# A hybrid mixer layer on one core: first group's solve levels moved, first rows loaded ahead of weights, weights split by whole blocks

## The chip, the core and the metric

The kernel runs on one core of one Trainium2 chip. The metric is device time in microseconds (us) of one execution. The kernel before was run three times: 2560.08, 2561.3 and 2566.76 us, median 2561.3. One more execution was taken with the hardware profiler: 2558.94 us.

A core has five engines with a queue of instructions each: TensorE (PE, matmuls, with its weight loads shown as PEld), VectorE (DVE), ScalarE (ACT), GpSimd (POOL) and SyncE (SP). Here SP issues most DMA transfers; ACT issues some too. An instruction that waits holds up all that stands behind it in its engine's queue.

## The reference

One layer of a streaming encoder: 2048 prompt rows (16 tiles of 128) and 128 sample rows (8 streams of 16, one more tile), width 1024.

```
h   = RMSNorm_pre(x);  P = h @ w_in   # [q|k|v (3*512) | z 512 | b 4 | a 4 | B 512 | C 512 | H 512]
q,k,v = SiLU(causal_conv4(..)); q,k L2-normed; beta = sigmoid(b); g = -exp(A_log)*softplus(a+dt)
per 64-row chunk, 4 heads of 128:
  A   = strictly lower (beta k k^T * decay);  [u|w] = (I + A)^-1 [beta v | beta k exp(g)]
  v_new = u - w S;  o = (q exp(g)) S + (q k^T * decay) v_new;  S = S*a_last + k_tail^T v_new
o   = RMSNorm_head(o) * SiLU(z)
y   = B * causal_conv3(C * H)
x   = x + RMSNorm_post(concat(o, y) @ w_o)
x   = x + RMSNorm_post2(SwiGLU(RMSNorm_pre2(x)))        # d_ff = 2816
```

All is fp32. The outputs are y for prompt and samples, and the new conv and delta-rule states.

## The kernel before

An fp32 matmul is made of three float32r matmuls: each operand is split into a rounded high part and a low rest, and wh·hi, wh·lo and wl·hi are summed. Making the parts is ACT's and DVE's work: ACT rounds a weight tile to `wh` (L276), DVE subtracts for `wl` (L277); rows are split by L212 (ACT, `hi`) and L213 (DVE, `lo`).

The kernel has four stages. In the mixer stage (0 to 943 us of the span) the 17 tiles go in five groups, `GROUPS = [[0,1,2],[3,4,5,6],[7,8,9,10],[11,12,16],[13,14,15]]` (16 is the sample tile). Each group runs through 28 column blocks of `w_in`, of 128 columns each. A block is 24 matmuls (8 slices of 128 rows, three each) into one PSUM bank, and its result goes through the convolutions and gates. Afterwards come the product with `w_o` (`o_tile`), the gate and up products, and the down product; the change doesn't touch the last two.

In group 0 (and for every fourth block in group 1) a block's weights come raw from `w_in`, are split, and the split pair (1 MB) is stored to a DRAM tensor `wsplit`; later groups load the pair from there. The pair sits in `w2`, a ring of three buffers; the raw tile `wr` (L275) comes as two halves of 128x512, from a ring of four. `fetch()` issues the next block's weights: once per block at its end, and at the very start in three calls between the first rows.

Before group 0 the rows `xs0` are loaded (L863, 8 slices, into tiles named `U` and `AU`), split, squared (L869 to L873), and their squares summed on TensorE (L881); the inverse norm is spread over the partitions by a TensorE transpose (L204) and scales everything that is read from a block's bank.

Everything that is not a block's matmuls (gate rates, decay masks, key products, the triangular solve, the chunks of the delta rule, loading and squaring of the next group's rows L225 to L235) is placed by `plan` between the thirds of the blocks: a block's matmuls come in three parts (9, 9 and 6), and `at(t, f)` puts `f` behind third number `t`. Distances in time are turned into thirds by `after(us)`, with 2.3 us a third in group 0 and `THIRD = {3: 1.95, 4: 2.5}` by the group's number of tiles in the others. TensorE's instructions stay in that written order. The order on the other engines is made by a scheduler.

The solve: `solve` forms the inverse of 32x32 diagonal blocks on DVE by pairs of small operations (L568, L570) on the transposed matrix `As` (L559). `solve_store` transposes the result into `utd` (L575, L576). Then `level_a` (L590, small matmuls with `utd`, L593), `level_b` (L607, L608), `level_c` (L629) and `level_d` (L640) combine the blocks, each a few TensorE instructions with DVE and ACT work between. `chunk` then runs the delta rule over the tiles; L699 is one of its matmuls, yt by dt, into an `obank`.

PSUM has eight banks: three `dbank` (blocks), two `tbank` (transposes, L342), two `gbank` (solve) and one `obank`. `out_turn` (L656) transposes a tile's result, in an `obank`; DVE reads it and multiplies by the gate (`ot`, L658); ACT issues the store to `mixo` (L659). The short convolution's result `yo` (L420) is stored to `mixs` by ACT's queue (L425).

The `w_o` stage begins with weights and rows that were loaded early (L976, L977 split them into `woh`, `wol`; L981, L982 split those loaded later, whole tiles of 128x1024). For each tile L1001 and L1002 split the mixer's rows `mh` and `ml`, and L1007 multiplies.

Of the kernel before, what the change touches and what calls it, by code (L numbers as in the profile page):

```python
# [17 lines left out]
P = 128  # L18
# [63 lines left out]
def kernel(  # L82
# [74 lines left out]
    with ExitStack() as ph:  # L157
# [21 lines left out]
        mark = {}  # L179
        early_w, early_m = [], []  # L180

# [27 lines left out]
        def split(xk, k, c, hi, lo):  # L209
            h = hp.tile([P, W1], F32R, tag="hi", name="hi")  # L210
            l = hp.tile([P, W1], F32R, tag="lo", name="lo")
            A.activation(h[:, :c], xk[:, :c], AF.Copy, scale=g_pre[:, k:k + 1])  # L212
# [50 lines left out]
        def weights(j, gi):  # L263
# [3 lines left out]
            if not (gi <= late or (gi == RAWG and j % 2)):  # L267
# [3 lines left out]
                return wh, wl  # L271
            for q in range(2):
                c = slice(4 * q, 4 * q + 4)
                wr = wp.tile([P, KD // 2, P], F32, tag="wr", name="wr", bufs=4)
                wload = nc.sync.dma_start(out=wr, in_=w_in[j, :, c])  # L275
                A.copy(wh[:, c], wr)  # L276
                V.tensor_tensor(out=wl[:, c], in0=wr, in1=wh[:, c].bitcast(F32), op=ALU.subtract)  # L277
            wloads.append(wload)
# [75 lines left out]
        def finish_block(j, ps, g):  # L354
# [62 lines left out]
            if kind == "B":  # L417
                acc = g["acc"]
                yo = cp.tile([P, W1], F32, tag="cs", name="yo")
                V.tensor_mul(yo[:, :pc], acc[:, :pc], ps[:, :pc])  # L420
# [232 lines left out]
        def out_turn(g, i, o):  # L653
            ps = obank()
            for h in range(H):
                T.transpose(ps[:, h * P:(h + 1) * P], o[:, h, :], ident)  # L656
            ot = wk.tile([P, H, P], F32, tag="ot", name="ot")
            V.scalar_tensor_tensor(ot, h4(ps), g_hd, g["sz"][:, :, i * P:(i + 1) * P], op0=ALU.mult, op1=ALU.mult)  # L658
            nc.scalar.dma_start(out=mixo[g["tiles"][i]], in_=ot)  # L659

# [106 lines left out]
        def plan(g, nx, events):  # L767
# [91 lines left out]
        hi, lo, sqs = [], [], []  # L859
        firsts = [psd.tile([P, 512], F32, tag="d", name="dbank") for _ in range(2)]  # L860
        for k in range(KD):
            raw = (U if k < 4 else AU)[:, k % 4].rearrange("p h c -> p (h c)")[:, :c]
            nc.sync.dma_start(out=raw, in_=xs0[k])  # L863
            split(raw, k, c, hi, lo)
            if k in (0, 3):
                fetch()
            sq = xbuf()
# [15 lines left out]
        rx = rstd(small, psn[:, :2 * n].rearrange("p (t c) -> p t c", c=2)[:, :, 0], n, 1.0 / D, EPS, "x")  # L883
        fetch()
        late()
        cw = gp.tile([P, 12, 4], F32, name="cw")
# [84 lines left out]
        for k in range(KD):  # L971
# [6 lines left out]
            else:  # L978
                wr = op.tile([P, D], F32, tag="xo", name="wor", bufs=2)
                nc.sync.dma_start(out=wr, in_=w_o[k])  # L980
                A.copy(wh, wr)  # L981
                V.tensor_sub(wl, wr, wh.bitcast(F32))  # L982
        nc.sync.dma_start(out=gpost, in_=rows_[0].partition_broadcast(P))

# [556 lines left out]
```

## Time and profile before

| | before |
|---|---|
| runs, us | 2560.08, 2561.3, 2566.76 (median 2561.3) |
| profiled execution, us | 2558.94 |
| its span, us | 2557.1 |
| mean granted TensorE clock | 0.99 |
| PE / DVE / ACT / POOL busy | 97 / 65 / 38 / 24 % |
| mixer stage ends (last block's matmul) | 943.3 us |

The span is the time from the first to the last recorded instruction. What the profile gives as "idle before" an instruction is the gap on its engine; the name behind the arrow is the instruction whose end released it. In the tables of waits a row is: engine, what waited (output and line), what it waited for, then total us, number of times, longest. In a timeline a row is: start in us, busy us, engine, line, operation, output and inputs, shape, and in brackets the idle time before it with its releaser. An engine name with a q is that engine's queue issuing something, such as a DMA.

### The profile page before, as it was taken

What the parts mean: (1) busy time and instruction counts of PE and PEld (TensorE: products, weight loads), DVE (VectorE), ACT (ScalarE), POOL (GpSimd) and SP (SyncE); (2) the same over time, 40 slices, a digit from 0 to 9 for tenths busy, and PEclk for the clock granted to TensorE, in tenths of its full rate; (3) what the DMA queues carried; (4) which work ended last, traced back from release to release, by engine and by line L of the source; (5) the groups of instructions that cost most, each with busy time, mean ns of one, the idle gap of its engine ahead of it and who ended that gap; (6) DMA issues with size and microseconds to landing.
All of it is one profiled execution on the core that took longest, in us unless ns stands there. A gap on an engine that the chain in (4) does not pass through costs nothing.

```text
span 2557.1 us, 39320 instructions
## 1 busy us (share of the span) xinstructions
PE 2469.6 (97%) x14366; PEld 2254.5 (88%) x14366; DVE 1667.9 (65%) x3106; ACT 976.7 (38%) x2095; POOL 607.3 (24%) x679
## 2 busy tenths in 40 slices
PE   7789999999999999999999999999999999999998
PEld 6788887888999988789999999999999987887786
DVE  6866755745755655768877764544655464677698
ACT  5435424423424323534433442222433345333343
POOL 1111010110111000215655500000000045455564
PEclk9989999999999999999999999999999999999999
DMA  6756554556667555669877888887888844333375
GB/s 231 256 209 220 180 206 179 180 172 205 232 223 254 207 182 189 210 227 340 285 261 263 283 267 262 262 252 260 284 282 294 280 152 127 95 124 123 125 226 183
DMA packets 287393, 561.91 MB, mean 220 GB/s; under 512 B 26652, under 2 KB 175328, under 8 KB 269920
## 3 DMA queue, kind: packets, MB, share of 16 engines
q1 hardware_dynamic: 165808, 483.06, 55.8%
q10 hardware_dynamic: 121392, 76.34, 9.6%
q8 instruction: 113, 1.85, 0.3%
q14 instruction: 80, 0.66, 0.1%
HBM read 400.62 MB, written 158.70 MB: 219 GB/s over the span
## 4 chain that ended last, share of the span: by engine, by line
PE 78%; DVE 11%; DMA 4%; issue 3%; ACT 2%; POOL 1%; ACTq 0%; SPq 0%; DVEq 0%; POOLq 0%
PE fbank L1223 32%; PE dbank L297 21%; PE fbank L1381 12%; PE tbank L1007 3%; PE dbank L1007 3%; DVE acc L1340 1%; DMA xt<-in_x 1%; PE tbank L342 1%; DVE acc L301 1%; DVE xr L1400 1%; PE obank L699 1%; DMA partd<-pt 1%; PE gbank L734 1%; POOL dw L1080 1%; PE obank L679 1%
## 5 line engine op out<-in xcount | busy, mean ns | idle before, releaser
L1223 PE MATMUL fbank<-xh,fw 128*128 128x384 f32 (+1 forms) x3696 | 899.2, 326 | 6.6 <-ACT m L1257 2.9
L297 PE MATMUL dbank<-hi,w 128*128 128x384 f32 (+1 forms) x2240 | 675.7, 369 | 10.7 <-ACT w L276 7.7
L1223 PEld LDWEIGHTS fbank<-xh,fw 128*128 128x128 f32 x3696 | 651.8, 188 | 8.3 <-ACT m L1257 3.6
L1223 PE MATMUL fbank<-xl,fw 128*128 128x384 f32 (+1 forms) x1848 | 602.5, 326 | 0.0
L1381 PE MATMUL fbank<-dw,as 128*128 128x512 f32 x1980 | 459.5, 393 | 8.6 <-DVE as L1365 2.7
L297 PEld LDWEIGHTS dbank<-hi,w 128*128 128x128 f32 x2240 | 418.9, 190 | 49.0 <-ACT w L276 7.6
L1381 PEld LDWEIGHTS fbank<-dw,as 128*128 128x128 f32 x1980 | 370.2, 188 | 97.7 <-DVE as L1365 4.1
L297 PE MATMUL dbank<-lo,w 128*128 128x384 f32 (+1 forms) x1120 | 404.0, 361 | 0.9 <-DVE lo L213 0.9
L1223 PEld LDWEIGHTS fbank<-xl,fw 128*128 128x128 f32 x1848 | 347.5, 188 | 0.0
L1365 POOL TENSOR_TENSOR as<-ar,as 128x256 fp32r<-128x256 f32 (+1 forms) x207 | 186.7, 912 | 277.1 <-ACT as L1362 276.4
L297 PEld LDWEIGHTS dbank<-lo,w 128*128 128x128 f32 x1120 | 213.7, 191 | 19.4 <-DVE lo L213 2.6
L1340 DVE TENSOR_TENSOR acc<-acc,fbank 128x512 f32<-128x512 f32 x248 | 166.1, 682 | 93.3 <-PE fbank L1381 75.6
L1080 POOL TENSOR_TENSOR dw<-dr,dw 128x512 fp32r<-128x512 f32 x52 | 76.8, 1489 | 484.7 <-ACT dw L1078 484.5
L1362 ACT CAST as<-ar 128x256 fp32r<-128x256 f32 (+1 forms) x288 | 118.1, 427 | 183.3 <-PE fbank L1381 135.6
L301 DVE SCALAR_TENSOR_TENSOR acc<-R,cw,acc 128x384 f32<-128x384 f32 (+2 forms) x180 | 121.2, 675 | 58.8 <-ACT acc L331 51.8
L1198 ACT CAST fw<-rg 128x512 fp32r<-128x512 f32 x124 | 77.4, 624 | 192.1 <-PE fbank L1223 154.4
L1270 DVE TENSOR_TENSOR c<-u,fbank 128x384 f32<-128x384 f32 (+1 forms) x66 | 34.8, 528 | 103.5 <-PE fbank L1223 103.4
L1266 DVE TENSOR_TENSOR m<-m,m 128x384 f32<-128x384 f32 (+1 forms) x44 | 23.1, 525 | 91.2 <-ACT m L1259 91.1
L1268 ACT ACTIVATE m<-fbank 128x384 f32<-128x384 f32 (+1 forms) x66 | 31.3, 474 | 127.6 <-PE fbank L1223 119.0
L1199 POOL TENSOR_TENSOR fw<-rg,fw 128x512 fp32r<-128x512 f32 x44 | 69.7, 1583 | 32.9 <-ACT fw L1198 32.8
L323 POOL COPY hist<-R 128x3 f32<-128x3 f32 x60 | 21.3, 355 | 190.3 <-ACT R L306 164.0
L1199 DVE TENSOR_TENSOR fw<-rg,fw 128x512 fp32r<-128x512 f32 x80 | 56.4, 706 | 15.3 <-ACT fw L1198 12.9
(359 smaller groups left out, 3476.3 us busy)
## 6 DMA issues: line engine op xcount, KB each, us to landing
w<-wsplit SPq DMA_DIRECT2D x105, 1024.0 KB, 4.9
fw<-fsplit SPq DMA_DIRECT2D x188, 512.0 KB, 4.8
fsplit<-fw SPq DMA_DIRECT2D x94, 512.0 KB, 4.2
partd<-pt ACTq DMA_DIRECT2D x88, 384.0 KB, 6.7
rg<-in_w_gu SPq DMA_DIRECT2D x62, 512.0 KB, 4.1
wsplit<-w SPq DMA_DIRECT2D x28, 1024.0 KB, 5.1
ar<-partd SPq DMA_DIRECT2D x48, 384.0 KB, 3.3
wr<-in_w_in SPq DMA_DIRECT2D x70, 256.0 KB, 5.0
```

The costliest lines, as they stand in the source:

```text
L297: T.matmul(ps[:, :c], l[:, k, :], r[k][:, :c], start=(k == 0 and r is hi and l is wh), stop=(k == KD - 1 and l is wl))
L301: r = V.scalar_tensor_tensor(acc, raw(d), w[:, d:d + 1], acc, op0=ALU.mult, op1=ALU.add)
L1007: T.matmul(pss[n], m_[:, j, :], w_[k][:, n * 512:(n + 1) * 512], start=(k == 0 and ci == 0), stop=(k == KD - 1 and ci == 2))
L1080: e.tensor_tensor(out=w[:, 1], in0=v, in1=w[:, 0].bitcast(F32), op=ALU.subtract)
L1198: A.copy(w[:, 0], v)
L1199: e.tensor_tensor(out=w[:, 1], in0=v, in1=w[:, 0].bitcast(F32), op=ALU.subtract)
L1223: T.matmul(ps, w_[:, c], b_[k][:, :hw], start=(first and k == 0 and ci == 0), stop=(k == KH - 1 and ci == 2), skip_group_check=not first)
L1270: V.tensor_add(c21, u2, b3)
L1340: V.tensor_add(dst, dst, ps)
L1362: ins = A.copy(a[:, 0, :n], v)
L1365: e.tensor_tensor(out=a[:, 1, :n], in0=v, in1=a[:, 0, :n].bitcast(F32), op=ALU.subtract)
L1381: T.matmul(ps, a[:, x_, q * P:(q + 1) * P], w[:, y_], start=(start and q == 0 and ci == 0), stop=(q == c - 1 and ci == 2), skip_group_chec ...
```

## The change

1. In group 0 the four levels stand seven thirds later. In groups of three tiles (0, 3 and 4) `level_b` stands 5 us behind `level_a` instead of 3.4, one third more; the rest follows.
2. At the start all eight row loads are issued in one go: the first block's weights behind the first slice, the second block's behind all eight. The squares come in a second loop. The other inputs (constants, convolution weights, caches, gate parameters, all by ACT's queue) are issued behind the last `hi` split.
3. A block's raw weights come as one tile of 128x1024, split by one ACT and one DVE instruction; only the first block is still done in halves. `wr` has two whole buffers in place of four halves.
4. `out_turn` transposes into a `tbank` in place of the `obank`.
5. The last group's last `mixs` store and the last tile's `mixo` store go from ACT's queue to SP's, behind the loads of `w_o`; the last `yo` gets another buffer.

On TensorE, group 0, around `level_a` of the kernel before (w_1251 is a block's weights, vraw a block of values being transposed, utd the solve's result, AU the matrix it multiplies):

```order
L297 MATMUL dbank<-lo,w_1251 128x384
L297 MATMUL dbank<-hi,w_1251 128x384
L342 MATMUL tbank<-cst,vraw 128x128 x3
L590 MATMUL gbank<-utd,AU 32x32 x24
L297 MATMUL dbank<-hi,w_1251 128x384
```

In the changed kernel the transposes of that block stand alone, and L595 (the same `level_a`) comes in a block two further on:

```order
L298 MATMUL dbank<-lo,w_1293 128x384
L298 MATMUL dbank<-hi,w_1293 128x384
L595 MATMUL gbank<-utd,AU 32x32 x24
L298 MATMUL dbank<-hi,w_1293 128x384
L298 MATMUL dbank<-lo,w_1293 128x384
```

Between the two places lie 57 block matmuls and three transposes.

On DVE, the last steps of group 0's solve before, and what stands around them (xt are squares of the next group's rows):

```order
L568 TENSOR_TENSOR pr<-As,Ts 128x108
L570 TENSOR_TENSOR Ts<-Ts,pr 128x9x12
L568 TENSOR_TENSOR pr<-As,Ts 128x96
L570 TENSOR_TENSOR Ts<-Ts,pr 128x8x12
L568 TENSOR_TENSOR pr<-As,Ts 128x91
L570 TENSOR_TENSOR Ts<-Ts,pr 128x7x13
L233 TENSOR_SCALAR xt,xss<-xt 128x512
L568 TENSOR_TENSOR pr<-As,Ts 128x78
L570 TENSOR_TENSOR Ts<-Ts,pr 128x6x13
```

After, the same steps (L573 and L575 are the solve's pair):

```order
L573 TENSOR_TENSOR pr<-As,Ts 128x108
L575 TENSOR_TENSOR Ts<-Ts,pr 128x9x12
L233 TENSOR_SCALAR xt,xss<-xt 128x512
L278 TENSOR_TENSOR w_1387<-wr,w_1387 128x1024
L573 TENSOR_TENSOR pr<-As,Ts 128x96
L302 TENSOR_SCALAR acc<-u,scw,acc 128x384
L575 TENSOR_TENSOR Ts<-Ts,pr 128x8x12
L302 TENSOR_SCALAR acc<-u,scw,acc 128x384
L573 TENSOR_TENSOR pr<-As,Ts 128x91
L233 TENSOR_SCALAR xt,xss<-xt 128x512
L575 TENSOR_TENSOR Ts<-Ts,pr 128x7x13
```

More of the blocks' own work stands between the solve's steps. Counted from `As` to `utd`: 9 weight subtractions of 128x1024 in place of 14 of 128x512, and in addition two taps of 128x384 (L302 with scw), one `vt`, one `cs`, one `u`, one `xt` square, one spread of 128x512 (L201) and two tiny ones.

The start of SP's queue before (U and AU take the rows, wr raw weights):

```order
L863 DMA U<-in_xs 128x384
L275 DMA wr<-in_w_in 128x512 x2
L863 DMA U<-in_xs 128x384 x3
L275 DMA wr<-in_w_in 128x512 x2
L282 DMA wsplit_82<-w_224 128x2048
L863 DMA AU<-in_xs 128x384 x4
L275 DMA wr<-in_w_in 128x512 x2
```

And after:

```order
L874 DMA U<-in_xs 128x384
L276 DMA wr<-in_w_in 128x512 x2
L874 DMA U<-in_xs 128x384 x3
L874 DMA AU<-in_xs 128x384 x4
L276 DMA wr<-in_w_in 128x1024
L283 DMA wsplit_82<-w_220 128x2048
L276 DMA wr<-in_w_in 128x1024
```

The four `AU` loads no longer stand behind the store of the first split block, nor behind the second block's weights.

```diff
-            for q in range(2):
-                c = slice(4 * q, 4 * q + 4)
-                wr = wp.tile([P, KD // 2, P], F32, tag="wr", name="wr", bufs=4)
-                wload = nc.sync.dma_start(out=wr, in_=w_in[j, :, c])
-                A.copy(wh[:, c], wr)
-                V.tensor_tensor(out=wl[:, c], in0=wr, in1=wh[:, c].bitcast(F32), op=ALU.subtract)
+            wr = wp.tile([P, KD, P], F32, tag="wr", name="wr", bufs=2)
+            parts = 1 if wloads else 2
+            for q in range(parts):
+                c = slice(KD // parts * q, KD // parts * (q + 1))
+                wload = nc.sync.dma_start(out=wr[:, c], in_=w_in[j, :, c])
+                A.copy(wh[:, c], wr[:, c])
+                V.tensor_tensor(out=wl[:, c], in0=wr[:, c], in1=wh[:, c].bitcast(F32), op=ALU.subtract)
...
-                nc.scalar.dma_start(out=mixs[g["gi"]][:, h, :], in_=yo[:, :c])
+                if last:
+                    last_stores.append((mixs[g["gi"]][:, h, :], yo[:, :c]))
+                else:
+                    nc.scalar.dma_start(out=mixs[g["gi"]][:, h, :], in_=yo[:, :c])
...
         def out_turn(g, i, o):
-            ps = obank()
+            ps = tbank()
...
+            if not gi:
+                t += 7
             for f in (level_a, level_b, level_c, level_d):
                 at(t, f, g)
-                t += after(3.4)
+                t += after(5 if f is level_a and n < MAXT else 3.4)
...
             nc.sync.dma_start(out=raw, in_=xs0[k])
+            raws.append(raw)
+            if not k:
+                fetch()
             split(raw, k, c, hi, lo)
-            if k in (0, 3):
-                fetch()
+        fetch()
+        for k, raw in enumerate(raws):
             sq = xbuf()
...
+        inputs = ExitStack()
+        inputs.enter_context(tc.issue_after(started))
         late()
...
+        inputs.close()
...
+        for a, b in last_stores:
+            nc.sync.dma_start(out=a, in_=b)
```

More of the change, by code (lines that the diff above doesn't have):

```diff
@@ L179 @@
         mark = {}
-        early_w, early_m = [], []
+        early_w, early_m, last_stores = [], [], []
         inner = ph.enter_context(ExitStack())
@@ L211, in split @@
             l = hp.tile([P, W1], F32R, tag="lo", name="lo")
-            A.activation(h[:, :c], xk[:, :c], AF.Copy, scale=g_pre[:, k:k + 1])
+            mark["hi"] = A.activation(h[:, :c], xk[:, :c], AF.Copy, scale=g_pre[:, k:k + 1])
             V.scalar_tensor_tensor(l[:, :c], xk[:, :c], g_pre[:, k:k + 1],
@@ L418, in finish_block @@
                 acc = g["acc"]
-                yo = cp.tile([P, W1], F32, tag="cs", name="yo")
+                last = h == 3 and g["gi"] + 1 == len(GROUPS)
+                yo = wk.tile([P, W1], F32, tag="ye", name="yo") if last else cp.tile([P, W1], F32, tag="cs", name="yo")
                 V.tensor_mul(yo[:, :pc], acc[:, :pc], ps[:, :pc])
@@ L658, in out_turn @@
             V.scalar_tensor_tensor(ot, h4(ps), g_hd, g["sz"][:, :, i * P:(i + 1) * P], op0=ALU.mult, op1=ALU.mult)
-            nc.scalar.dma_start(out=mixo[g["tiles"][i]], in_=ot)
+            if i + 1 < g["npr"] or g["gi"] + 1 < len(GROUPS):
+                nc.scalar.dma_start(out=mixo[g["tiles"][i]], in_=ot)
+            else:
+                last_stores.append((mixo[g["tiles"][i]], ot))
         def tail_keys(g, i):
@@ L860 @@
         firsts = [psd.tile([P, 512], F32, tag="d", name="dbank") for _ in range(2)]
+        raws = []
         for k in range(KD):
@@ L884 @@
         fetch()
+        started = mark["hi"].ins
+        inputs = ExitStack()
+        inputs.enter_context(tc.issue_after(started))
         late()
```

## The prediction, made before the changed kernel ran

> **What bounds the kernel now.** I read the page first: busy shares, TensorE's row in 40 slices, the granted clock.
>
> ```profile
> span 2557.1 us, 39320 instructions
> PE 2469.6 (97%) x14366; PEld 2254.5 (88%) x14366; DVE 1667.9 (65%) x3106; ACT 976.7 (38%) x2095; POOL 607.3 (24%) x679
> PE   7789999999999999999999999999999999999998
> PEclk9989999999999999999999999999999999999999
> ```
>
> TensorE is the bound; 2557.1 − 2469.6 = 87.5 us of the span lie between its matmuls. A slice is 64 us, and only the first three and the last are not full. So all that this change can win is idle time of TensorE, mostly in the first 192 us, and it adds no matmul. The waits of TensorE over the whole span name the places.
>
> ```profile
> engine line waited for: us in total, times, longest us
> PE gbank L590 <- DVE utd L575: 14.2, 2, 13.9
> PE obank L699 <- DVE ot L658: 7.8, 7, 2.1
> PE dbank L297 <- ACT w L276: 7.7, 1, 7.7
> ...
> PE dbank L1007 <- ACT mh L1001: 5.9, 2, 3.7
> ...
> PE gbank L607 <- ACT xs L593: 2.3, 1, 2.3
> ```
>
> Five parts of the change each aim at one of these rows. I take them in the order of the program.
>
> **The start.** The timeline of the first 31 us:
>
> ```profile
> 2.11 2.71 SPq L863 DMA_DIRECT2D U<-in_xs  x3
> 7.00 1.26 ACT L276 CAST w<-wr 128x512 fp32r<-128x512 f32 x2
> 7.65 0.69 PE L297 MATMUL dbank<-hi,w 128*128 128x384 f32 x1 [7.65 <-ACT w L276]
> 9.79 5.72 SPq L863 DMA_DIRECT2D AU<-in_xs  x4
> 14.71 0.20 ACT L901 ACTIVATE nega<-al 128x4 f32<-128x4 f32 x1 [2.60 <-DMA al<-in_gates]
> 15.65 0.61 ACT L212 ACTIVATE hi<-AU,vec 128x384 fp32r<-128x384 f32 x1
> 16.31 0.69 PE L297 MATMUL dbank<-hi,w 128*128 128x384 f32 x1 [2.86 <-ACT hi L212]
> 30.49 1.48 PE L204 MATMUL tbank<-xk,cst 128*128 128x384 f32 x2
> ```
>
> The rows of the second half (AU) are issued only at 9.79, behind the store of the first split block, which itself waits for DVE's subtraction. So the first block, begun at 7.65, stands in its middle until 16.31. ACT, which must split those rows, spends 2.6 us waiting for `al`, a small gate input.
>
> In the changed kernel SP issues the AU rows right behind U's three, at about 2.11 + 2.71 = 4.8 us. All rows (8 x 196 KB), the first weights (512 KB) and the start's other loads had this rate to come at:
>
> ```profile
> 4.00:6.00 2.00, 0.00 (x0) 0.00 (x0) 0.00 (x0) 1.23 (x1) 0.00 (x0) 1.00 0.95 323
> ```
>
> At 323 GB/s, 2.1 MB need 6.5 us; with some 2 us ahead of the first byte the rows are there at about 8.5. ACT then has eight `hi` at 0.61, three squares at about 0.5 and two half casts (1.26), 7.7 us from about 6, so the last `hi` ends near 13.7 and the first block near 14.5. The second block's weights now wait for ACT: behind the last `hi` stand three DMA issues and one whole cast. They are ready near 17, the block ends near 21, and L204 stands near 25 in place of 30.49: 5.5 us. Against that, `al` is still issued from ACT's queue, ahead of the third block's cast, and the fourth block's cast and subtraction (1.05 + 1.23, whole tiles, below) now stand ahead of the first taps. I take 1.5 off: **4 us**, bounds 1 (ACT's queue gives most of it back) and 7 (L204 at 23.5, no loss).
>
> What the rate is under two queues the trace shows in part: in that window the engines are 95% busy. The Trainium skill, "DMA: Bandwidth & Descriptors", section "Queues, rings and completion order", says that a DMA engine takes turns between its queues packet by packet; by it, moving ACT's constants behind the last `hi` gives the rows a larger share of the engines, which would put the start's gain nearer to 5.5. The row of 323 GB/s agrees with busy engines, and no row separates the queues' shares.
>
> **Levels of group 0.** The largest single hole, with DVE's prices in the first 160 us:
>
> ```profile
> 91.99 2.12 DVE L559 STREAM_TRANSPOSE As<-pk 128x1024 f32<-128x1024 f32 x1 [2.76 <-ACT pk L557]
> 120.99 0.55 PE L342 MATMUL tbank<-cst,vraw 128*128 128x128 f32 x3
> 134.38 1.06 DVE L575 STREAM_TRANSPOSE utd<-Ts 128x512 f32<-128x512 f32 x1
> 135.49 1.49 PE L590 MATMUL gbank<-utd,AU 32*32 32x32 f32 x48 [13.95 <-DVE utd L575]
> L277 DVE TENSOR_TENSOR w<-wr,w 128x512 fp32r<-128x512 f32 x44 | 30.2, 704 | 8.1 <-ACT w L276 7.9
> L301 DVE SCALAR_TENSOR_TENSOR acc<-R,cw,acc 128x384 f32<-128x384 f32 x36 | 21.7, 610 | 2.6 <-ACT acc L333 1.9 <-POOL hist L323 0.5
> L233 DVE SCALAR_TENSOR_TENSOR xt<-xt 128x512 f32<-128x512 f32 x4 | 2.7, 687 | 2.2 <-DMA xt<-in_x 2.2
> ```
>
> TensorE reaches the level at 121.54, that is 29.55 us behind the start of `As`; `utd` ends 43.45 us behind it (135.44). Seven thirds later means 57 more block matmuls, by the order. A block's 24 matmuls and three transposes take 4.85 us here (two such transposes start at 116.14 and 120.99), so 57 and three need some 10.3: TensorE arrives at +39.85. But TensorE's extra blocks bring DVE extra work, which the scheduler puts between the solve's steps: nine whole subtractions for fourteen halves, 9 x 1.23 − 14 x 0.704 = 1.2 us (the 1.23 is a whole subtraction, row below); two taps, 1.2; `vt`, `cs` and `u` at 0.55, 1.65 (as `yo`, of the same shape, in the last timeline below); one square 0.69 and one spread, also 128x512, 0.69; a little for two tiny ones: 5.7 us. `utd` then ends at +49.15, and the remaining hole is 9.3 us. A fourth square joins the three whose loads DVE waited 2.2 us for, so I leave 10: the gain is **4 us**, not the 13.95 that the move might suggest. Bounds: 0 (the squares wait longer, `As` itself comes later) and 6.9 (those 2.2 us gone: 7.1 left).
>
> Behind the hole the clock drops:
>
> ```profile
> 120.00:140.00 20.00, 5.91 (x66) 5.29 (x66) 13.16 (x41) 7.91 (x18) 0.78 (x3) 0.60 0.53 186
> 136.91 0.69 PE L297 MATMUL dbank<-hi,w 128*128 128x384 f32 x1
> 141.21 0.34 PE L297 MATMUL dbank<-lo,w 128*128 128x384 f32 x1
> ```
>
> Thirteen matmuls start from 136.91 up to 141.21, 0.33 us apart, where those ahead start (4.85 − 0.55)/24 = 0.18 apart: 13 x 0.15 = 1.9 us. With 10 us of hole left I save none of it. "TensorE: Matmul & The Clock Gate" of the Trainium skill, section "Part 1: The HAM clock gate", lets the clock fall after about 3.4 us of idle time; by that, the 1.9 us would come on top only with the hole under 3.4. The trace agrees so far that 13.95 us drop it (granted clock 0.60).
>
> **Level b in groups of three.** L607 waits 2.3 us, once, for `xs`; nine more matmuls stand ahead of it: 9 x 0.18 = **1.6 us**, bounds 0 and 2.3.
>
> **Outputs in transposition banks.** DVE's reading of the output bank, over the mixer stage (min/median/max in ns):
>
> ```profile
> L658 DVE SCALAR_TENSOR_TENSOR ot<-obank,vec,sz x17: 743/746/753, 179.9 to 942.2; 128x512 f32<-128x512 f32 x17
> ```
>
> L699 waits 7.8 us in seven places for DVE's reading of the one `obank`. With `out_turn` elsewhere that reader is gone. A transpose (L342) may now find its `tbank` held by the output until `ot` has read it, 0.75 us a time; there are two banks, and the row for `obank` counts seven of 17 tiles as late. I take **7 us**, bounds 2 (each of seven waits turns into up to 0.75 us on a `tbank`, and one in ten is new) and 7.8.
>
> **Whole-block splits.** Rows on both sides:
>
> ```profile
> L276 ACT CAST w<-wr 128x512 fp32r<-128x512 f32 x44 | 25.7, 617 | 34.9 <-PE dbank L297 19.6 <-DMA wr<-in_w_in 9.6 <-issue 4.8
> 953.30 1.05 ACT L981 CAST woh<-wor 128x1024 fp32r<-128x1024 f32 x1 [3.35 <-DMA wor<-in_w_o]
> 954.38 1.23 DVE L982 TENSOR_TENSOR wol<-wor,woh 128x1024 fp32r<-128x1024 f32 x1 [2.89 <-ACT woh L981]
> ```
>
> Whole is cheaper on the engines (1.05 for 2 x 0.617, 1.23 for 2 x 0.704). A block's weights become ready later by half a cast and half a load, some 1.5 us, and a load now needs a whole tile free. The cover is the ring of three: before, ACT's cast mostly waits for TensorE to give a buffer back (19.6), not for the load (9.6), and after the start TensorE waits for no `w`. **0**, bounds −3 and +25 us (third rival).
>
> **The end of the mixer stage.**
>
> ```profile
> 943.30 0.55 DVE L420 TENSOR_TENSOR yo<-acc,dbank 128x384 f32<-128x384 f32 x1 [0.30 <-PE dbank L297]
> 944.27 0.62 ACT L976 CAST woh<-U 128x512 fp32r<-128x512 f32 x1 [4.37 <-DVE yo L420]
> 944.92 0.69 DVE L977 TENSOR_TENSOR wol<-U,woh 128x512 fp32r<-128x512 f32 x1 [1.06 <-ACT woh L976]
> 947.02 0.79 PE L1007 MATMUL dbank<-woh,mh 128*128 128x512 f32 x1 [3.75 <-ACT mh L1001]
> 947.33 0.68 DVE L1002 TENSOR_TENSOR ml<-vt,mh 128x512 fp32r<-128x512 f32 x1
> 948.89 0.63 PE L1007 MATMUL dbank<-woh,ml 128*128 128x512 f32 x1
> ```
>
> ACT stands at the store of `yo` until 944.27, and its casts behind it. With both stores on SP it can cast ahead, and TensorE starts 3.75 us earlier. But DVE still does `yo`, then four `wol` (0.69 each), then `ml`: 943.85 + 2.75 + 0.68 = 947.3 at best, so the first matmul with `ml` moves only from 948.89 to about 947.7: **1.2 us**, bounds 0 and 4. On SP the stores stand ahead of gpost and the mixer rows (two issues, 0.33 each); nothing there is due at once.
>
> **Sum.** 4 + 4 + 1.6 + 7 + 0 + 1.2 = 17.8 us: 2558.94 − 17.8 = 2541.1 for an execution like the profiled one, which is 2.4 below the median; so 2543 as a median.
>
> **The rivals.** (1) *The hole all but closes.* DVE fills with the solve what it left idle between 120 and 140 us, 20 − 13.16 = 6.8. The hole falls from 9.3 to 2.5, a gain of 11.4 in place of 4; if the clock then stays up, 1.9 more: 2534 to 2536. For it: DVE's idle time there. Against: that idle time lies between steps of one chain, where DVE waits for TensorE or for a load, and the order puts the blocks' work in between.
> (2) *The gains are moved, not won.* TensorE reaches each level sooner after a faster start, and DVE, whose solve is what ends last, is no earlier: the start's 4 us become 4 us of hole, level a gains nothing, and the tbank's waits eat 5 of 7. Left are 2 + 1.6 + 1.2, about 5: 2556. For it: the 13.95 is DVE's chain, not TensorE's place. Against: `As` hangs on TensorE's key products and moves with the start.
> (3) *Slower: the whole-block loads become the bound in the two raw groups.* A `wr` is free only when its subtraction has ended; two blocks' cycle is load to landing (5.0 us at the median for halves, up to 7.0), cast 1.05, subtraction 1.23 and DVE's queue ahead of it, some 2: 9.5 us, or 4.75 a block, against TensorE's 4.85. It decides from 10.9 us a cycle on: then the 28 blocks of group 0 lose 28 x 0.6 = 17 us. At 11.5 they lose 25, and the time is 2561 + 25 − 18 = 2568.
>
> ```profile
> DMA to landing us min/median/max: 2.5/5.0/7.0
> 100.00:120.00 20.00, 18.09 (x109) 17.46 (x107) 19.76 (x53) 7.68 (x15) 4.22 (x6) 1.00 0.97 353
> ```
>
> For it: a load twice as large, engines 97% busy at 100 to 120, DVE full. Against: ACT's casts wait mostly on TensorE.
>
> **How the numbers follow.** Two executions differ by some 0.3% (7.7 us) before they can be told from no change; faster is below 2553.6. Forecast 0.62 (own range 2536 to 2551, the terms' bounds taken half at a time), rival (1) 0.10, rival (2) 0.16, of which a third still reads as faster, rival (3) 0.12, of which a quarter ends within 0.3%. Faster: 0.62 + 0.10 + 0.05 = 0.77; same: 0.11 + 0.03 = 0.14; slower 0.09. The range from 2531 to 2558 leaves out rival (3) and little more.
>
> **What would show it.** L204 near 25 us; L595 waiting 9 to 11 us for `utd`; no row of L707 (the former L699) waiting for `ot`; no wait of L298 for `w` after 30 us; the first matmul with `ml` 1 to 1.5 us sooner after the last block. It is wrong if waits on `w` show in the first 300 us, if the wait for `utd` is 14 again, or if L343 waits in `tbank` for `ot`.

## The result and the profile after

The changed kernel takes 2541.9 us (median of four runs, 2538.53 to 2544.14), the kernel before 2562.8 (median of four, 2560.08 to 2566.76): a ratio of 0.9916, 95% interval 0.9898 to 0.9934. The forecast was 2543. Its own profiled execution took 2544.14 us, with a span of 2542.4, so it is 14.7 us shorter in span than the one of before.

```profile
span 2542.4 us, 39159 instructions
PE 2466.6 (97%) x14366; PEld 2255.2 (89%) x14366; DVE 1664.0 (65%) x3072; ACT 976.6 (38%) x2061; POOL 608.1 (24%) x679
PE   7889999999999999999999999999999999999997
PEclk9999999999999999999999999999999999999999
```

TensorE's busy time is nearly the same (2466.6 for 2469.6). Most of what is gone is time between its matmuls: 75.8 us are left of 87.5. The row of tenths shows it only in slice two (64 to 128 us); the short waits further on are too small for it. From the table of waits of TensorE, over the whole span:

```profile
PE tbank L343 <- ACT qT L336: 8.7, 5, 4.3
PE gbank L595 <- DVE utd L580: 8.4, 2, 8.2
PE dbank L298 <- ACT w L277: 5.9, 1, 5.9
...
PE tbank L895 <- DVE xk L884: 3.4, 1, 3.4
...
PE gbank L742 <- DMA st<-in_state: 2.2, 1, 2.2
...
PE gbank L612 <- ACT xs L598: 1.7, 1, 1.7
PE dbank L1027 <- DVE ml L1022: 1.5, 2, 1.3
```

The 7.8 us of waiting for `ot` have gone without a successor in the `tbank`. The wait for `utd` went from 13.9 to 8.2. Of the waits that are new or larger, two are taken up below: 3.4 us for a square of the first rows (0.9 before), and 2.2 us for the sample tile's state (none before).

To follow the gain through the kernel I use one mark: the start of DVE's last `yo` (the short convolution's output) in each group, the instruction of L422 (L420 before). Last `yo` of groups 0 to 4: 212.4, 414.7, 615.9, 785.4, 943.3 us before; 203.0, 401.4, 598.8, 768.6, 925.4 after. So 9.4 us are won in group 0, 3.9 in group 1, 3.7 in group 2, −0.2 in group 3, 1.1 in group 4: 17.9 in all. The first gate/up matmul (L1223, now L1243) comes 17.9 us sooner too (1151.6 to 1133.7). Of this, the profiled execution gives 3.4 back in the gate and up stage, which the change doesn't touch. Over all 14 traces of this study, the time from the first L1243 to the first matmul of the down stage lies between 924.6 and 928.8 us, with the same code. So the total time can't tell what a part of a few microseconds is worth.

The marks are better, but not good to a microsecond everywhere. Where the code is the same, group 2 takes 197.44 to 197.45 us in eleven traces and group 4 takes 156.83 to 156.85 in nine. Group 3 takes 168.7 to 172.1 us in the five traces that have the changed kernel's code there. Part of this scatter is the granted clock. Behind a wait of about 2 us it fell in some traces and not in others. An example is the wait for the sample tile's state, in the kernel with the levels put back and in the one with the old start (both below; timelines from 720 to 740 us):

```profile
722.82 3.42 PE L742 MATMUL gbank<-st,kz 128*128 128x128 f32 x16 [2.41 <-DMA st<-in_state]
721.72 2.02 PE L742 MATMUL gbank<-st,kz 128*128 128x128 f32 x16 [2.48 <-DMA st<-in_state]
```

The waits are alike, but the same 16 matmuls took 1.4 us longer in the first. The granted clock was 0.59 and 0.56 from 722 to 726 us there, and 1.00 from 722 to 724 in the second. In the same way, behind a wait for `vraw` near 110 us (1.7 to 2.4 us long), the clock fell to 0.50 in six of the 14 traces, the changed kernel's among them, and stayed at 1.00 in eight. So a difference of 1 to 3 us at the last `yo`, from one trace of each kernel, shows nothing unless the place where it arises is found.

The start after, in the timeline of the first 28 us:

```profile
3.75 1.82 SPq L874 DMA_DIRECT2D AU<-in_xs  x4
5.95 0.69 PE L298 MATMUL dbank<-hi,w 128*128 128x384 f32 x1 [5.95 <-ACT w L277]
14.61 0.34 ACTq L917 DMA_DIRECT2D al<-in_gates  x1
18.42 0.52 ACT L887 ACTIVATE xk<-AU 128x384 f32<-128x384 f32 x1 [4.99 <-DMA al<-in_gates]
22.25 1.44 PE L895 MATMUL tbank<-cst,xk 128*128 128x1 f32 x6 [3.37 <-DVE xk L884]
27.54 0.86 PE L204 MATMUL tbank<-xk,cst 128*128 128x384 f32 x2
```

The AU rows are issued at 3.75 us instead of 9.79, and from 8.8 us on TensorE runs through the first block and half of the second. Then ACT stands at its queue of held-back inputs, from the end of a cast at 13.4 until 18.4, and a square of the first rows stands behind it.

The level of group 0:

```profile
88.77 2.12 DVE L564 STREAM_TRANSPOSE As<-pk 128x1024 f32<-128x1024 f32 x1 [2.77 <-ACT pk L562]
139.06 1.17 PE L595 MATMUL gbank<-utd,AU 32*32 32x32 f32 x36 [8.19 <-DVE utd L580]
```

TensorE arrives at 139.06 − 8.19 = 130.87, 42.1 us behind `As`; `utd` is there 50.3 us behind it.

And the end of the mixer stage:

```profile
925.40 0.55 DVE L422 TENSOR_TENSOR yo<-acc,dbank 128x384 f32<-128x384 f32 x1 [0.99 <-PE dbank L298]
927.11 0.50 PE L1027 MATMUL dbank<-woh,mh 128*128 128x512 f32 x1 [1.31 <-ACT mh L1021]
929.68 0.79 PE L1027 MATMUL dbank<-woh,ml 128*128 128x512 f32 x1 [1.31 <-DVE ml L1022]
```

### The profile page after: what moved, and what is told of

Same layout as the page of the kernel before. It is cut to its first block, busy times and chain, and to the rows that moved or that the text cites. A ratio compares the mean times of both kernels' runs of the same rounds, so it can differ in the third digit from the quotient of the medians.

```text
span 2542.4 us, 39159 instructions
## 1 busy us (share of the span) xinstructions
PE 2466.6 (97%) x14366; PEld 2255.2 (89%) x14366; DVE 1664.0 (65%) x3072; ACT 976.6 (38%) x2061; POOL 608.1 (24%) x679
## 4 chain that ended last, share of the span: by engine, by line
PE 79%; DVE 10%; DMA 5%; issue 3%; ACT 3%; POOL 1%; ACTq 0%; SPq 0%; DVEq 0%; POOLq 0%
PE fbank L1243 33%; PE dbank L298 21%; PE fbank L1401 11%; PE tbank L1027 3%; PE dbank L1027 3%; DVE xr L1420 1%; PE tbank L343 1%; DVE acc L1360 1%; DMA wr<-in_w_in 1%; POOL dw L1100 1%; DMA partd<-pt 1%; DVE acc L302 1%; DVE w L278 1%; PE gbank L742 1%; PE gbank L693 1%
## 5 line engine op out<-in xcount | busy, mean ns | idle before, releaser
L1243 PE MATMUL fbank<-xh,fw 128*128 128x384 f32 (+1 forms) x3696 | 900.1, 327 | 8.6 <-ACT m L1277 4.9
L1243 PEld LDWEIGHTS fbank<-xh,fw 128*128 128x128 f32 x3696 | 653.0, 188 | 10.1 <-ACT m L1277 5.6
L1243 PE MATMUL fbank<-xl,fw 128*128 128x384 f32 (+1 forms) x1848 | 603.3, 326 | 0.0
L1243 PEld LDWEIGHTS fbank<-xl,fw 128*128 128x128 f32 x1848 | 348.1, 188 | 0.0
L298 PEld LDWEIGHTS dbank<-lo,w 128*128 128x128 f32 x1120 | 213.6, 191 | 18.4 <-DVE lo L213 1.7
L302 DVE SCALAR_TENSOR_TENSOR acc<-R,cw,acc 128x384 f32<-128x384 f32 (+2 forms) x180 | 121.2, 675 | 54.5 <-ACT acc L332 48.7
```

Source lines behind the costliest of these rows:

```text
L298: T.matmul(ps[:, :c], l[:, k, :], r[k][:, :c], start=(k == 0 and r is hi and l is wh), stop=(k == KD - 1 and l is wl))
L302: r = V.scalar_tensor_tensor(acc, raw(d), w[:, d:d + 1], acc, op0=ALU.mult, op1=ALU.add)
L1243: T.matmul(ps, w_[:, c], b_[k][:, :hw], start=(first and k == 0 and ci == 0), stop=(k == KH - 1 and ci == 2), skip_group_check=not first)
```

## Experiments: each part undone

Five kernels undo one part of the change each; line numbers differ by a few where lines were put in or taken out. The reference mark is the last `yo` of the changed kernel, 925.40.

**Levels back at their place.**

```diff
-            if not gi:
-                t += 7
```

> The changed kernel with the levels of group 0 back at their old place (no seven thirds). Theory A (the hole is DVE's chain from As to utd against TensorE's arrival, and the shift won only what DVE's extra work left of it): seven whole weight subtractions for fourteen halves make the chain 1.25 us shorter than in the kernel before, so TensorE waits 12 to 13 us for utd (8.2 in the changed kernel, 13.9 before), and the last block's yo, which starts at 925.4 us in the changed kernel, comes 4 to 5 us later; the time rises by 4 to 5 us. Rival B (the hole shrank because of the earlier start and the cheaper splits, not because of the shift): it stays at 8 to 10 us and the last yo within 2 us of 925.4.

```profile
132.21 1.49 PE L595 MATMUL gbank<-utd,AU 32*32 32x32 f32 x48 [13.34 <-DVE utd L580]
931.16 0.55 DVE L422 TENSOR_TENSOR yo<-acc,dbank 128x384 f32<-128x384 f32 x1 [1.00 <-PE dbank L298]
```

The wait is back at 13.3, a little over A's 12 to 13, and the last `yo` 5.8 us later. Of these 5.8 us, 3.4 are there at the end of group 2; the other 2.4 arise in group 3, where the edit changes nothing and the clock fell in this trace (above). The time was 2547.3 us (ratio to before 0.9935, 0.992 to 0.995). Theory A: the shift made the hole smaller, by 5.2 us, half of the 10.3 us by which it moved the level; the earlier start and the cheaper subtractions leave the hole nearly as it was.

**Outputs back in the output bank.**

```diff
-            ps = tbank()
+            ps = obank()
```

> The changed kernel with out_turn back in the one obank. Theory A (all seven waits were in the path): L707 waits 7 to 8 us for ot again, and the last yo comes 7 to 8 us later than 925.4. Rival B (part of what those waits took was made up elsewhere, in waits that come a little later anyway): the waits are back at 7 to 8, the last yo moves by 4 or less. The milestones of the yo say in which group.

The waits of TensorE from 250 to 960 us, and the last `yo`:

```profile
PE obank L707 <- DVE ot L663: 6.4, 7, 1.8
PE gbank L742 <- DMA st<-in_state: 2.4, 1, 2.4
PE gbank L634 <- DVE AU L619: 2.3, 1, 2.3
939.42 0.56 DVE L422 TENSOR_TENSOR yo<-acc,dbank 128x384 f32<-128x384 f32 x1 [1.14 <-PE dbank L298]
```

Together with 2.2 us before 250 us, the waits for `ot` are 8.6, a little over A's 7 to 8; but the last `yo` is 14.0 us later, more than either theory gave. The `yo` at the groups' ends show where: 0.8, 5.1, 9.0, 13.5 and 14.0 us behind the changed kernel's, so 3.9 to 4.5 in each of groups 1 to 3. In group 1 the waits of L707 are three, 3.0 us together, and the group takes 4.3 us more. The timelines show what the rows leave out. One tile's transposes (L661), its waiting L707 and the block matmul behind it, in this kernel:

```profile
367.07 0.60 PE L661 MATMUL obank<-cst,o 128*128 128x128 f32 x4
370.00 1.16 PE L707 MATMUL obank<-yt,dt 128*128 128x128 f32 x8 [1.44 <-DVE ot L663]
370.92 0.48 PE L298 MATMUL dbank<-hi,w 128*128 128x512 f32 x1
```

And the same place in the changed kernel:

```profile
365.32 0.60 PE L661 MATMUL tbank<-cst,o 128*128 128x128 f32 x4
367.46 0.47 PE L298 MATMUL dbank<-hi,w 128*128 128x512 f32 x1
```

From the first transpose to the block matmul it is 3.85 us for 2.14, so 1.71 us for a row of 1.44. The row counts only the idle time behind the modelled end of the matmuls ahead. Unhindered, L707 starts 0.17 us before that end and takes 0.10 us less. At the eleven places where L707 follows a tile's transposes, two of them without a row, the excess over 2.14 us adds up to 11.6 us for 8.6 in the rows. The rest of the 14.0 is not this part's own: `As` came 1.2 us sooner in this trace, and group 3 took 3.9 us more than its one place accounts for, with a wait of L634 of 2.3 us and a clock that fell to 0.50 behind it. The time was 2554.3 us (0.9966, 0.9952 to 0.9981).

**Weights by halves again.**

```diff
-            wr = wp.tile([P, KD, P], F32, tag="wr", name="wr", bufs=2)
-            parts = 1 if wloads else 2
-            for q in range(parts):
+            for q in range(2):
+                c = slice(4 * q, 4 * q + 4)
+                wr = wp.tile([P, KD // 2, P], F32, tag="wr", name="wr", bufs=4)
...
```

> The changed kernel with the weights split by halves again. Theory A (hidden but for DVE's chain in the hole): 18 halves at 0.704 for 9 wholes at 1.23 make the chain from As to utd 1.6 us longer, the wait for utd 9.5 to 10 us, the last yo 1 to 2 us later; no wait of TensorE for weights in either. Rival B (nothing at all, the terms drown): last yo within 0.5 us. Rival C (half loads come earlier, and so does everything at the start): L204 1 us or more before 27.5 and the last yo earlier.

```profile
25.15 1.08 PE L204 MATMUL tbank<-xk,cst 128*128 128x384 f32 x2
141.07 1.49 PE L594 MATMUL gbank<-utd,AU 32*32 32x32 f32 x48 [8.67 <-DVE utd L579]
926.44 0.56 DVE L421 TENSOR_TENSOR yo<-acc,dbank 128x384 f32<-128x384 f32 x1 [0.99 <-PE dbank L297]
```

L204 is 2.4 us earlier, as rival C had it, but the last `yo` is 1.0 us later. The wait for `utd` grew by 0.5 us, not by the 1.3 to 1.8 of A. At the end of group 2 it is 2.0 us later, 1.7 of it from a later `As`. That this part is worth anything is not shown (time 2542.2; 0.9921, 0.9902 to 0.994, no difference from the changed kernel). No row of TensorE names a wait for weights beyond the first block, here or in the changed kernel.

**Start in the old order.** The row loop with its two weight fetches and squares as before, and the inputs not held back:

```diff
-            if not k:
-                fetch()
             split(raw, k, c, hi, lo)
-        fetch()
-        for k, raw in enumerate(raws):
+            if k in (0, 3):
+                fetch()
...
-        inputs.enter_context(tc.issue_after(started))
```

> The changed kernel with the start's order as before (weights between the rows, squares in the rows' loop, inputs not held back). Theory A (the start's gain is kept to the end): L204 near 30.5 instead of 27.5 us, the wait for utd still about 8, the last yo 3 us later than 925.4. Rival B (a faster start only makes the hole of the level larger): the wait for utd falls to about 5 and the last yo stays within 1 us.

```profile
142.96 1.49 PE L595 MATMUL gbank<-utd,AU 32*32 32x32 f32 x48 [8.15 <-DVE utd L580]
928.66 0.56 DVE L422 TENSOR_TENSOR yo<-acc,dbank 128x384 f32<-128x384 f32 x1 [1.01 <-PE dbank L298]
```

Theory A: L204 at 31.1 us, the wait for `utd` unchanged at 8.1, the last `yo` 3.3 us later (3.7 at the end of group 2). The start's gain is kept through the hole, since `As` moves with it (92.6 for 88.8). Rival B, the half of the prediction's second rival that is about the start, falls with this. The time was 2546.7 us (0.9933, 0.9911 to 0.9956).

Undone one by one, these four parts sum to 5.8 + 14.0 + 1.0 + 3.3 = 24.1 us at the last `yo`, where 17.9 were won. At the end of group 2 they sum to 18.1 us, where 17.1 were won. So most of the surplus is group 3's, and does not show that the parts depend on each other.

**Level b at its old distance.**

```diff
-                t += after(5 if f is level_a and n < MAXT else 3.4)
+                t += after(3.4)
```

> The changed kernel with level_b back at 3.4 us behind level_a in groups of three tiles. Theory A (that third brought what its row says, but put the sample tile's first state load behind a block's weights on SP's queue): L612 waits 2 to 3 us in group 0, 3 or 4 for xs, L742's wait of 2.2 us for the state is gone, and the last yo is 1 to 2 us earlier than 925.4: this part cost. Rival B (the prediction's): L612 waits 2.3 again and the last yo is 1 to 2 us later.

```profile
PE gbank L612 <- ACT xs L598: 3.3, 1, 3.3
925.47 0.55 DVE L422 TENSOR_TENSOR yo<-acc,dbank 128x384 f32<-128x384 f32 x1 [0.30 <-PE dbank L298]
```

Neither theory: the last `yo` stays (925.47 for 925.40). The wait for `xs` is 1.6 us longer, that for the state is gone; at the ends of groups 0 to 2 this kernel is 1.9 to 3.0 us ahead (0.9 of it from an earlier `As`), and it loses 1.2 of this in group 3, where the clock is 0.98 for 1.00, and 0.75 in group 4. In group 4, which repeats so closely, the third is thus worth 0.75 us; over the whole stage it brings nothing and costs nothing that these traces can tell. The time was 2543.8 us (0.9919, 0.9897 to 0.9942).

Putting the last stores back on ACT's queue was not tried alone.

## Experiments: one part alone on the kernel before

**Output banks alone**, the one line `ps = tbank()` in the kernel before.

> The kernel before with one part of the change alone: out_turn in a tbank. Its waits for ot were 7.8 us. Undone from the changed kernel this part cost 14.0 us at the last yo, with 8.6 us of waits for ot and a new 2.3 us wait of L634. Theory A (a wait of TensorE costs more than its row shows, about 1.4 times, since the pipeline of weight loads and matmuls starts anew behind it): the last yo comes 10 to 12 us before 943.3. Rival B (the rows are the whole price): 7 to 8 us. Rival C (the part is worth the same in either kernel): 13 to 14 us.

```profile
930.89 0.55 DVE L420 TENSOR_TENSOR yo<-acc,dbank 128x384 f32<-128x384 f32 x1 [0.30 <-PE dbank L297]
```

12.4 us before 943.30, 11.7 when counted from `As` (which came 0.7 us sooner). Theory A has the size. Added up place by place as above, the kernel before took 10.7 us over 2.14 us each at eleven places: the seven with a row 9.7 us for 7.8 (0.27 us more each), and four without a row 1.0 us. In the kernel with the one word changed, every such place takes 2.14 us. No row of a `tbank` grew in the first 250 us but L342's for kT, by 0.7. The time was 2550.0 us (0.9949, 0.993 to 0.9967): the larger part of the whole gain comes from this one word.

**Levels alone**, `t += 7` in the kernel before.

> The kernel before with the seven thirds alone. Theory A (TensorE arrives 10.3 us later by its extra blocks and DVE has 1.6 us more of half subtractions than the changed kernel in the chain): the wait for utd is 9 to 10 us, the last yo 4 to 5 us before 943.3. Rival B (the part needs the later output banks: with chunks pushed later into one obank its gain is lost): the wait falls just so, and the last yo moves by less than 2 us.

```profile
140.82 1.49 PE L590 MATMUL gbank<-utd,AU 32*32 32x32 f32 x48 [8.89 <-DVE utd L575]
938.88 0.55 DVE L420 TENSOR_TENSOR yo<-acc,dbank 128x384 f32<-128x384 f32 x1 [0.30 <-PE dbank L297]
```

The last `yo` is 4.4 us sooner, as A has it, with a wait just under A's 9 to 10, and B falls: the part does without the other banks. (One execution, 2558.2 us.)

## Experiments: what stays late

**Inputs behind the last square.**

```diff
-        started = mark["hi"].ins
+        started = mark["sq"].ins
```

where `mark["sq"]` is the last of ACT's squares.

> The changed kernel with the other inputs held back behind ACT's last square instead of its last hi. In the changed kernel ACT stands idle from 13.4 to 18.4 us at the issue of al and the issues behind it, the last square behind them, and TensorE waits 3.4 us for it (L895). Theory A (that queue is what kept the start from its 4 us): the wait at L895 falls under 1 us, L204 comes at 23.5 to 25 us instead of 27.5, the last yo 2.5 to 3.5 us before 925.4. Rival B (what comes late next, the inputs themselves and the third block's weights, takes it back): L204 earlier, but As and the last yo within 1 us.

```profile
23.75 0.81 PE L204 MATMUL tbank<-xk,cst 128*128 128x384 f32 x2
29.68 0.50 PE L152 MATMUL gbank<-hi,wba 128*16 128x384 f32 x1 [5.12 <-DVE wba L930]
924.07 0.55 DVE L422 TENSOR_TENSOR yo<-acc,dbank 128x384 f32<-128x384 f32 x1 [1.00 <-PE dbank L298]
```

The square's wait is gone (0.9), and L204 comes 3.8 us earlier, but `wba`, made from one of the inputs that were held back further, is late next and takes 5.1 us. The last `yo` is 1.3 us earlier, close to what B had, and no more than the scatter. The time was 2545.6 us (0.9931, 0.9916 to 0.9946), not below the changed kernel's.

**First state load one third earlier**, which puts it ahead of a block's weights on SP:

```diff
-                    thread((u - (2 if h else 0), u, u + 3, u + 5, u + 7, u + 9), sample_head(g, npr, h))
+                    thread((u - (2 if h else 1), u, u + 3, u + 5, u + 7, u + 9), sample_head(g, npr, h))
```

> The changed kernel with the first state load of the sample tile one third earlier, which puts it ahead of a block's 1 MB of weights on SP's queue. In the changed kernel L742 waits 2.2 us for it, a wait that the kernel before hadn't. Theory A (a new wait out of the changed places in the queue): the wait is under 0.3 us and the last yo 2 to 3 us before 925.4. Rival B (the weights behind it come late in turn): a wait of L298 for weights of 1 us or more, the last yo unchanged.

```profile
922.30 0.56 DVE L422 TENSOR_TENSOR yo<-acc,dbank 128x384 f32<-128x384 f32 x1 [0.99 <-PE dbank L298]
```

The row of L742 is gone, no wait for weights appears, and the last `yo` is 3.1 us earlier, 2.8 of it won in group 3, where the edit acts. The four traces with this edit take 165.4 to 168.3 us in group 3, the five without it 168.7 to 172.1. Theory A, though how much of it is the clock is open. The time was 2540.7 us (0.9914, 0.9899 to 0.9929). The next three kernels have this edit in them.

**`wba_r` first of the inputs**, those behind the last square:

```diff
         inputs.enter_context(tc.issue_after(started))
+        wba_r = gp.tile([P, KD, 8], F32, name="wba_r")
+        nc.scalar.dma_start(out=wba_r, in_=w_ba)
...
-        wba_r = gp.tile([P, KD, 8], F32, name="wba_r")
-        nc.scalar.dma_start(out=wba_r, in_=w_ba)
```

> The changed kernel with the earlier state load, the inputs behind ACT's last square and wba_r as the first of them. With the inputs behind the square alone, L204 came 3.8 us earlier, but L152 then waited 5.1 us for wba. Theory A (wba_r was the next late one): L152 waits under 1 us, As starts 2.5 to 4 us earlier than 88.8 to 90.2, the last yo 2 to 4 us before 922.3. Rival B (again another input is late, cw or the gates): L204 near 24 and As within 1 us of 89.

The longest wait of ACT in its first 40 us:

```profile
ACT w L277 <- DMA gbia<-in_gates: 6.2, 1, 6.2
```

L152 waits no longer, L204 is at 24.6, and `As` starts at 89.5: rival B. The weights' cast now stands 6.2 us behind the issue of `gbia`. Whatever stands behind the small inputs on ACT's queue is late; the trace shows the place, not what the issues themselves wait for. The last `yo` came at 920.89, 1.4 us before 922.3, again no more than the scatter; the time was 2537.8 us (0.989, 0.9869 to 0.9912).

**Levels seven thirds later still**, `t += 14` in place of `t += 7`.

> The changed kernel with the earlier state load and with the levels of group 0 fourteen thirds later instead of seven (against the run with the earlier state load alone: wait for utd 7.9 us, last yo 922.3). DVE's chain from As to utd takes in two more whole subtractions and three small operations, 4.1 us, TensorE arrives 10.3 us later. Theory A (the hole is the difference of the two): the wait for utd falls to 1 to 3 us, the granted clock stays up behind it, the last yo comes 6 to 8 us earlier. Rival B (the chunks of group 0, now later, lose it again at the group's end or in group 1): the wait falls just so, and the yo at the end of group 1 is earlier by 3 us or less.

```profile
141.70 0.95 PE L595 MATMUL gbank<-utd,AU 32*32 32x32 f32 x48
915.68 0.56 DVE L422 TENSOR_TENSOR yo<-acc,dbank 128x384 f32<-128x384 f32 x1 [0.99 <-PE dbank L298]
```

The wait for `utd` is gone entirely, and the last `yo` is 6.6 us before 922.3: theory A. At the end of group 0 the gain is 9.4 us (193.1 for 202.5), at the end of group 1 it is 5.1 (395.98 for 401.04), more than the 3 that rival B allows. The difference of 4.3 is no loss: a chunk of group 0 that stood ahead of its last `yo` now stands behind it (its last L707 at 208.3 us, 197.2 with the state load alone), and TensorE idles for 0.1 us or less in group 1 of both. The busy times from 120 to 140 us, of the changed kernel and of this one (TensorE, its weight loads, DVE, ACT, POOL, then the granted clock):

```profile
120.00:140.00 20.00, 11.58 (x98) 10.95 (x97) 17.80 (x50) 6.76 (x15) 1.86 (x4) 0.84 0.80 286
```

```profile
120.00:140.00 20.00, 18.12 (x101) 17.03 (x101) 17.64 (x48) 7.67 (x13) 1.87 (x4) 1.00 0.93 321
```

DVE is as busy in both; it is TensorE that has work. Three waits are new or longer in group 0 (L693 3.0 us for r, L634 1.8 for AU, L204 1.7 for the solve's steps), smaller together than the one that went. The time was 2539.8 us (0.9891, 0.9865 to 0.9917), which can't be told from the 2540.7 of the state load alone.

**Squares of group 1's rows all on ACT.**

```diff
-                with tc.issue_after(mark["V" if q else "A"].ins):
-                    if q:
+                dve = q and nx["to"] > 1
+                with tc.issue_after(mark["V" if dve else "A"].ins):
+                    if dve:
                         V.scalar_tensor_tensor(xt, xt, 1.0, xt, op0=ALU.mult, op1=ALU.mult, accum_out=acc)
```

`nx["to"]` is the number of the group that the rows are for.

> The changed kernel with the earlier state load and with the squares of group 1's rows all on ACT, so that DVE's chain loses four squares (0.69 each, and 1.1 us of waits for their loads) and the spread behind them. Theory A (the hole is DVE's chain): the wait for utd falls from 7.9 to 3 to 4 us, the last yo comes 4 to 6 us before 922.3. Rival B (DVE waits for something else in that time, its removed work is filled by waits): the wait stays above 6.

```profile
134.87 1.49 PE L596 MATMUL gbank<-utd,AU 32*32 32x32 f32 x48 [5.61 <-DVE utd L581]
920.89 0.56 DVE L423 TENSOR_TENSOR yo<-acc,dbank 128x384 f32<-128x384 f32 x1 [1.01 <-PE dbank L299]
```

`utd` is ready 3.7 us earlier than with the state load alone (134.9 for 138.6), but TensorE arrives 1.4 earlier too, and so the wait falls by 2.3 only, between A and B. Most of the 3.7 is not the squares': `As` itself came 3.0 us earlier, and counted from it `utd` is only 0.7 us earlier. Near 110 us the clock fell here and stayed up there; against the changed kernel, where it fell too, the chain from `As` to `utd` is 2.6 us shorter. The last `yo` came 1.4 us earlier, no more than the scatter. The time was 2536.8 us (0.9884, 0.9865 to 0.9903): the lowest median of the study, 5.1 us under the changed kernel, with intervals that overlap.

Each of the five kernels that add to the changed one takes less time than the kernel before (every interval lies under 1); by the times, none is shown to take less than the changed kernel. Whether the last two and the input order add up was not run.

## Why the prediction was right, point by point

The time (2541.9 for 2543), the sign and the sum to the end of the mixer stage (17.9 us for 17.8) came out. The terms did so less well, and their errors cancel: that the sum agrees to 0.1 us is luck.

- **Start, 4 us.** About 3: L204 at 27.5 us (26.2 to 27.5 in the traces with this start and whole blocks) for 30.5 (28.1 to 31.1 in the traces with the old one); undone 3.3 at the end. The mechanism held (AU rows at 3.75, first blocks through). Where the step failed is the place of ACT's input issues: I had them ahead of the third block's weights and forgot the square of the first rows behind them, which cost TensorE 3.4 us. L204 was put near 25. The rule on DMA queues that the prediction cited (the Trainium skill, "DMA: Bandwidth & Descriptors", section "Queues, rings and completion order") would have put the gain nearer to 5.5; the rows did come sooner than reckoned (the last `hi` ends at 11.5 us, reckoned 13.7), but no run here separates the queues' shares.
- **Levels, 4 us.** 4.4 alone, 5.8 undone (3.4 without group 3's scatter). The mechanism held. The two arrivals were reckoned at +39.85 and some +50 us from `As` and measured at +42.1 and +50.3; the hole, put at 10 us, is 8.2. TensorE arrived 2.3 us later than reckoned. Of this, 0.5 is a slip in the sum (the three transposes' 0.55 us were named but not added), and about 1.6 is the clock, which fell near 110 us in this trace; with the state load moved, where it stayed up, TensorE arrives at +40.5 and `utd` is there at +48.4. DVE's extra work, put at 5.7 us, shows there as 4.9 us (43.5 before). In the changed kernel DVE waits 1.4 us more for TensorE's blocks on the way. So the hole is about the same in both (8.2 and 7.9), and it was the difference of two late arrivals. The clock: the rule of the Trainium skill ("TensorE: Matmul & The Clock Gate", section "Part 1: The HAM clock gate") lets it fall after some 3.4 us of idle time. The traces agree for the long hole (0.50 from 134 us on, in the middle of the 8.2 us) and for no wait (1.00). For short waits they differ from it: the clock also fell behind waits of 1.9 to 2.4 us, and did not each time. So a hole under 3.4 us would not have been safe. What the clock alone is worth here was not measured.
- **Level b, 1.6 us.** About 0 (0.75 in group 4). The wait for `xs` fell from 2.3 to 1.7, and to 1.0 in most other runs, but the third moved the sample tile's state load behind a block's weights on SP: 2.2 us of new wait. I had counted the matmuls that moved and not the DMA that moves with them.
- **Output banks, 7 us.** 12.4 alone, 14.0 undone. This is the term that was mis-sized most, outside my bounds of 2 to 7.8. The price that I put on a row of waits was the row itself. Place by place it is the row and 0.27 us, and four places without a row cost 1.0 us: 10.7 us in all. The waits in the `tbank` that I feared did not come.
- **Whole-block splits, 0.** Not told from 0 (1.0 us at the last `yo`); rival (3) did not come: no wait for weights behind the first block.
- **End, 1.2 us.** From the last `yo` to the first matmul with `ml`: 5.59 us before, 4.28 after, so 1.3, as reckoned (the three traces with the old end have 4.8 to 5.6 us, those with the new one 3.6 to 4.3). But from the last `yo` to the first gate/up matmul both take 208.34 us, and over the runs this stretch lies between 203.9 and 209.1. Whether the 1.3 us is kept is open.
- **Rivals.** (1) did not come: the hole closed only with fourteen thirds. (2) had the right worry (the hole is DVE's chain) but the start's gain passes through it, as the run with the old start shows.

## What to carry to other kernels

Read a short wait of the bounding engine as more than its row when it recurs (time the whole place in both traces), and give the reader of a bank its own buffers first: the cheapest edit here brought most. When work is shifted to fill a hole, reckon both arrivals, since the shift brings its own work to the late engine; and follow the DMA issues that shift with it, on each queue. In a kernel whose untouched stages scatter by 4 us, judge a part at a mark just behind it, not by the total, and look first at how far stretches of unchanged code repeat. A stretch that takes longer with the same code is to be held against the granted clock before it is put down to an edit. A gain at a mark counts only if no work has slipped behind the mark.

## What had not been expected of the hardware

- Seven waits for `ot`, 7.8 us by the table, were worth 11.7 to 12.4 us. Each costs 0.27 us more than its row on average, since matmuls that follow each other without a wait overlap (by 0.17 us here) and those behind a wait take longer (0.92 us to the next start for 0.82). Places where the overlap is lost but nothing shows as idle cost 0.2 to 0.4 us each.
- The granted clock fell to 0.50 behind a wait of 1.9 to 2.4 us in six traces and stayed at 1.00 behind one of 1.7 to 2.2 in eight, at the same place of the code. Where it fell, the next blocks came about 1.6 us later.
- The start scatters by 2 us between executions of the same code: L204 at 30.5, 28.1 and 28.3 us with the old order of loads.
